# Attention in units of four key blocks, with paced row maxima, earlier output weights and operands loaded in place

## The chip, the cores and the metric

The program runs on one core of a Trainium2 chip (trn2). The metric is the device time of one execution in microseconds (us). A core has a matrix engine (TensorE, PE in the profile, with its weight loads as PEld), a vector engine (VectorE, DVE), a scalar engine (ScalarE, ACT) that also evaluates exp and tanh, a fourth engine (GpSimd, POOL) and a queue that issues the transfers between main memory and on-chip memory (SyncE, SP). Each engine takes its instructions in its program's order. Matmuls write to banks of PSUM; a "twin" is a pair of banks, one for each of the two heads that are worked together.

## The reference

One layer of a streaming encoder. After a modulated norm, one projection gives an S5 branch (a scan over the sequence and a gated linear unit, GLU) and an attention branch; both are gated, concatenated, and go through one output projection. The attention has 8 heads of 64, over a prompt of 2048 positions (causal) and over 64 new positions that see 512 cached ones.

```python
y_ssm = y_ssm * jax.nn.sigmoid(y_ssm @ w_glu.astype(f32) + b_glu.astype(f32))
y_ssm = (y_ssm * jax.nn.silu(z_s.astype(f32))).astype(x.dtype)
...
s = jnp.einsum('bqhd,bkhd->bhqk', q, k).astype(jnp.float32) * ATTN_SCALE
s = s + jnp.transpose(cum_q, (0, 2, 1))[:, :, :, None] - jnp.transpose(cum_k, (0, 2, 1))[:, :, None, :]
mask = pos_k[None, :] <= pos_q[:, None]
s = jnp.where(mask[None, None], s, -jnp.inf)
p = jax.nn.softmax(s, axis=-1)
return jnp.einsum('bhqk,bkhd->bqhd', p.astype(v.dtype), v)
```

## The kernel before

Four stages follow each other on PE: projections and scan (to 725 us), GLU (to 795), attention (to 1214), output product (to 1387). All matrix work is float32, made of products of a high and a low part.

**Attention** (class Attn) works on head pairs hp 0 to 3. Each has five query tiles: qt 0 to 3 of 512 prompt positions, and qt 4 for the new ones. `order` puts qt 4 first in each pair. A tile meets its key blocks of 128 keys; tile qt has 4·qt + 4 of them, and the last four (on the diagonal) are 512, 384, 256 and 128 queries wide. Each block passes through these steps, and the letters are used below:

- S, scores (`scores`): transposed scores (keys on partitions) in a twin, six matmuls in three pairs plus a pair (`sm`,`kb`) that adds the biases and subtracts the row maximum; ACT then writes exp into a block p (the `act` helper), and p is added to one of two running sums `acc` for the softmax's denominator, on DVE or POOL in turn (`i % 2`, recorded at L1489).
- V (`mix`): p times values into one PSUM bank, over all blocks of a tile. Two blocks (PVG = 2) make a unit; V of a unit is issued one unit later (`pend`).
- M, maxima (`maxima`): an upper bound of the next tiles' row maxima needs a coarse product q·k of 128 queries and up to 512 keys per twin, and DVE adds the biases `cb` and reduces (`pb`, `pm`, L1411; two per M). `run` issues one M after each S, whatever its size, while any are queued; their results go through a transpose (`identr`, `mq`) into `sm`.
- T (`turn`): PE transposes a loaded tile of k or q; ACT copies the high part, DVE subtracts for the low part (`ks`, `qs`, L1375).
- SUM (`sums`): the running sum's total over keys, its reciprocal, z (gate times result) and the store to `ma_d`.

PE's order is that of the code: the class Chain adds a dependency from each PE instruction to the one before. The other engines' order is set by a scheduler. PSUM holds three twins for S and M, one bank for V and one for T and SUM (`Banks`).

**GLU** (`Glu.mm`): 16 steps of 24 matmuls each. After ACT's tanh, two operations on DVE (L1663, L1664) form the product of the tanh, y and the gate. Two M and one T per step are put between (MXU = 2).

**Output** (class Out): `weights` is a generator that loads the 16 blocks of the output weights through a ring of three buffers `ost` (L1749), casts the high part on ACT (`ohb`, L319) and subtracts the low part on POOL (`olb`, L205). `run` of Attn advances it by two steps per unit, from the point at which no loads, transposes or maxima are left. Out.run then computes eight pairs of chunks with seven products each; `load`, `differ` and `split` bring, combine and split the operands of pair p; SP fetches stored weights (`t3`, `t4`) and residual rows x between them.

## Time and profile before

| | |
|---|---|
| median of 3 runs | 1392.0 us (1387.33 to 1394.06) |
| profiled execution, its own time | 1393.23 us |
| its span in the profile | 1391.4 us, 1.83 us outside |
| PE busy | 1312.5 us (94%) |
| DVE busy | 968.5 us (70%) |
| ACT busy | 652.0 us (47%) |
| POOL busy | 520.5 us (37%) |
| mean granted PE clock | 0.981 of full speed |

A busy time is the union of an engine's instructions; matmuls overlap in their pipeline, so the duration of one group of matmuls is longer than its distance to the next group's start. What a group costs on PE is therefore read from the starts of consecutive rows. In 795 to 1214.3, PE counts as busy for 400.77 of 419.30 us; a wait between two matmuls that is shorter than the pipeline's fill does not show as idle time.

### The profile page before, as it was taken

Reading aid. Unit: us, or ns where it says so; the run is one execution under the profiler, and the core shown is the slowest. Engines: PE = TensorE matmul, PEld = TensorE weight load, DVE = VectorE, ACT = ScalarE, POOL = GpSimd, SP = SyncE. Lnnn points to the kernel's source line nnn. Section 1 sums busy time; section 2 is a strip of 40 time slices with the busy share of each in tenths; the row PEclk is TensorE's granted clock in tenths of the full one; section 3 lists DMA queues with packets and bytes.
Section 4 is the critical chain, followed back from the end, with each engine's and each line's share of the span. In section 5 each row is a group of like instructions: output and inputs, shape, how many; then the busy total and the mean of one; then the engine's idle time right before and its main releaser. Section 6 shows DMA issues by size and latency. Waiting matters only on the chain.

```text
span 1391.4 us, 25886 instructions
## 1 busy us (share of the span) xinstructions
PE 1312.5 (94%) x9164; PEld 1031.9 (74%) x9164; DVE 968.5 (70%) x2404; ACT 652.0 (47%) x1710; POOL 520.5 (37%) x502
## 2 busy tenths in 40 slices
PE   5888999999999899999999899999999989898998
PEld 2886999998889899998879755555555554387887
DVE  3635896977877679864218877786787885446775
ACT  3645356567453576573315335445445445522211
POOL 1100254556534354452004113423423426743453
PEclk9899999999999999999999889999999999999999
DMA  9885333543546836446249624134121133495552
GB/s 342 318 309 124 100 86 94 154 123 107 163 133 217 282 110 180 145 141 196 84 138 291 202 73 121 32 91 125 43 70 48 40 65 79 146 330 169 182 164 78
DMA packets 249476, 204.92 MB, mean 147 GB/s; under 512 B 91296, under 2 KB 217340, under 8 KB 248322
## 3 DMA queue, kind: packets, MB, share of 16 engines
q1 hardware_dynamic: 249346, 203.27, 47.6%
q8 instruction: 72, 1.18, 0.4%
q14 instruction: 58, 0.48, 0.1%
HBM read 137.68 MB, written 65.53 MB: 146 GB/s over the span
## 4 chain that ended last, share of the span: by engine, by line
PE 63%; DVE 11%; DMA 6%; POOL 4%; issue 4%; ACT 3%; SPq 1%; DVEq 0%; ACTq 0%; POOLq 0%
PE low L154 25%; PE twin L154 13%; PE bank L154 12%; PE last L154 7%; PE glu L154 3%; DVE pb L1411 2%; PE bank L157 2%; DMA wst<-in_w_in_dram 1%; POOL qss L329 1%; POOL olb L205 1%; DMA lt<-t 1%; DVE acc L1489 1%; ACT p L354 1%; DVE ev L650 1%; DVE wlo L323 1%
## 5 line engine op out<-in xcount | busy, mean ns | idle before, releaser
L154 PE MATMUL low<-whi,h 128*128 128x256 f32 (+1 forms) x1584 | 296.3, 285 | 6.5 <-DVE th L609 3.5
L154 PE MATMUL low<-h,whi 128*128 128x256 f32 (+2 forms) x1152 | 277.6, 332 | 0.4 <-DVE h L323 0.3
L154 PEld LDWEIGHTS low<-whi,h 128*128 128x128 f32 x1584 | 247.9, 189 | 10.0 <-DVE th L609 3.7
L1411 DVE CUSTOM_DVE_ANT_0 pb<-twin,cb 128x512 bf16<-128x512 f32 (+3 forms) x328 | 199.9, 609 | 58.9 <-PE twin L154 49.1
L154 PE MATMUL low<-wlo,h 128*128 128x256 f32 (+1 forms) x816 | 229.1, 283 | 5.9 <-DVE wlo L323 5.9
L154 PEld LDWEIGHTS low<-h,whi 128*128 128x128 f32 x1152 | 195.5, 192 | 21.4 <-issue 2.8
L354 ACT ACTIVATE p<-twin 128x1024 f32<-128x1024 f32 (+3 forms) x180 | 149.7, 839 | 119.4 <-PE twin L154 107.2
L154 PE MATMUL low<-h,wlo 128*128 128x256 f32 (+2 forms) x576 | 188.2, 327 | 1.2 <-DVE wlo L323 1.2
L154 PEld LDWEIGHTS low<-wlo,h 128*128 128x128 f32 x816 | 154.3, 189 | 8.2 <-DVE wlo L323 7.7
L154 PE MATMUL bank<-p,vt 128*64 128x512 f32 (+3 forms) x704 | 142.5, 527 | 0.0
L154 PE MATMUL twin<-qs,ks 64*128 64x512 f32 (+3 forms) x1056 | 134.1, 359 | 0.0
L154 PEld LDWEIGHTS low<-h,wlo 128*128 128x128 f32 x576 | 110.3, 192 | 10.9 <-DVE wlo L323 2.6
L323 DVE TENSOR_TENSOR wlo<-wst,whi 128x512 fp32r<-128x512 f32 (+1 forms) x96 | 71.6, 752 | 59.9 <-ACT whi L319 59.7
L1489 DVE TENSOR_TENSOR acc<-acc,p 128x1024 f32<-128x1024 f32 (+4 forms) x88 | 90.2, 1025 | 30.5 <-ACT p L354 28.1
L329 POOL TENSOR_TENSOR qss<-qss,mhalf 128x4 f32<-128x4 f32 (+1 forms) x68 | 79.9, 1176 | 84.1 <-DVE qss L328 76.0
L154 PEld LDWEIGHTS twin<-qs,ks 64*128 64x128 f32 x1056 | 95.2, 191 | 11.0
L154 PE MATMUL twin<-sm,kb 64*128 64x512 f32 (+3 forms) x360 | 78.0, 428 | 21.2 <-DVE pm L1411 14.4
L319 ACT CAST whi<-wst 128x512 fp32r<-128x512 f32 (+1 forms) x96 | 58.7, 619 | 73.2 <-PE low L154 37.5
L154 PEld LDWEIGHTS bank<-p,vt 128*64 128x64 f32 x704 | 45.2, 140 | 63.8 <-issue 56.1
L205 POOL TENSOR_TENSOR x<-x,ot 128x512 f32<-128x512 f32 (+1 forms) x34 | 52.8, 1556 | 84.4 <-DVE ot L1816 79.7
L154 PEld LDWEIGHTS twin<-sm,kb 64*128 64x128 f32 x360 | 34.5, 187 | 61.8 <-DVE pm L1411 32.8
L646 ACT ACTIVATE hsq<-ev 128x64 bf16<-128x64 f32 (+1 forms) x272 | 69.7, 256 | 8.2
(437 smaller groups left out, 2634.2 us busy)
## 6 DMA issues: line engine op xcount, KB each, us to landing
wst<-in_w_in_dram SPq DMA_DIRECT2D x48, 512.0 KB
x<-in_x_prompt_dram SPq DMA_DIRECT2D x32, 512.0 KB
h<-h SPq DMA_DIRECT2D x16, 1024.0 KB
wada<-in_w_ada_dram SPq DMA_DIRECT2D x12, 1024.0 KB
cb<-cb_d SPq DMA_DIRECT2D x20, 512.0 KB
out_dram<-ev SPq DMA_DIRECT2D x64, 128.0 KB
out_dram<-x SPq DMA_DIRECT2D x32, 256.0 KB
z_d<-th SPq DMA_DIRECT2D x24, 256.0 KB
```

The source lines that it names most:

```text
L154: return self.keep(self.pe.matmul(*a, **kw))
L157: return self.keep(self.pe.transpose(*a, **kw))
L205: PL.tensor_tensor(out, x, y, op=op)
L319: i = S.copy(hi, x)
L323: V.tensor_tensor(lo, x, hi, op=ALU.subtract)
L329: PL.tensor_tensor(out, out, bc(mhalf[:out.shape[0]], list(out.shape)), op=ALU.pow)
L354: i = S.activation(out, x, func, **kw)
L646: S.activation(sq[:r], tv[:, h], AF.Square, accum_out=ss[:r, h:h + 1])
L650: V.tensor_tensor(tv, tv, e.bc(ss[:r].unsqueeze(2), [r, 4, HD]), op=ALU.mult)
L1411: V.tensor_tensor_reduce(b[:, :n], ps[:, h, :n], cb[:, h, :n], 1.0, NEG, ALU.add, ALU.max, accum_out=self.pm[:, t, h, pi:pi + 1])
L1489: (PL if j else V).tensor_tensor(y[:rows, :, c0:nq], x[:rows, :, c0:nq], p[:rows, :, :n], op=ALU.add)
```

## The change

Four parts, with the new names that matter.

**Units of four blocks.** PVG is 4, and V follows in the same unit, directly behind the unit's scores, with the blocks of the unit in order. The ring of p grows from 6 to 8 buffers, that of z from 2 to 3. The decode tile (qt 4) is no longer a row of units of its own: `decoded` makes its scores of four cached blocks in one twin with one exp, and it is joined to another unit (behind qt 1 for the first pair; with the last unit of the pair before for the others).

**Paced maxima.** `pace` issues an M only while DVE's estimated lag is below LAG or tiles need it: one at the head of a unit (none in the first unit), one in its middle, two behind its last scores. `biases` loads `cb` for each group of M (44 loads instead of 20, four buffers). Two transposes may share a twin (`turns`). The adds of a unit are issued behind its scores, three of eight on DVE and five on POOL (before, in turn), and smaller blocks may go to POOL too. DVE's order in attention is now pinned to the code's, by the same Chain class (so all its lines read L156).

**GLU.** The two DVE operations become two ACT operations, one POOL product (`pmul`) and one DVE product per step.

**Output weights and operands.** The weights start once nothing is left to load or transpose, though maxima may still be queued, with three steps per unit (four when no maxima are left), a ring of four, and the low part on DVE when no maxima are left. Operands of the first pairs are loaded in place, four `ot` instead of two; `load(2)` is issued before the residual's and `t4` fetches; decode's operands are split earlier.

```diff
-PVG = 2
+PVG = 4
 MXU = 2
+LAG = 4.6
...
-    def matmul(self, *a, **kw):
-        return self.keep(self.pe.matmul(*a, **kw))
-
-    def transpose(self, *a, **kw):
-        return self.keep(self.pe.transpose(*a, **kw))
+    def __getattr__(self, name):
+        f = getattr(self.pe, name)
+        return lambda *a, **kw: self.keep(f(*a, **kw))
...
+    V, PE = Chain(tc, nc.vector, nosync), Chain(tc, nc.tensor, nosync)
...
+            self.order += [(hp, qt) for qt in ((4, 0, 1, 2, 3) if hp else (0, 1, 4, 2, 3))]
...
+    def turns(self, two, apart):
+
+        n = self.due()
+        if n < 2 and not apart or not two:
+            return self.turn()
+        ps = self.twin()
+        self.evicts += [self.turned(False, ps[:, h]) for h in range(min(n, 2))]
...
+            if not self.can("cw" if new else "cb", 1):
+                return
+            w = DEC if new else 4 * P
+            t0 = 20 if new else 16 if kind == "c" else 4 * kind
+            cb = self.bias_at[j] = self.claim([P, 2, w], "cw" if new else "cb", j, F32)
+            e.nc.sync.dma_start(cb, e.cb_d[2 * hp:2 * hp + 2, t0 * P:t0 * P + w].partition_broadcast(P))
...
+    def pace(self, most=1):
+
+
+        for i in range(most):
+            if self.need <= 0 and self.lag >= LAG:
+                return i
+            n = self.maxima()
+            if not n:
+                return i
+            self.need -= 1
+            self.lag += 2 * n / 960 + 0.25 - n / 2400
+        return most
...
+        self.adds.append((tile, tile.n - 1, p, rows, c0, n))
+        return self.values[tile.hp, kd], t, rows, c0, n, p
+
+    def add(self, tile, i, p, rows, c0, n):
+
+        V, PL = self.e.V, self.e.PL
+        acc, nq = tile.acc, tile.nq
         whole = not c0 and rows == P
         late = tile.end and i >= tile.nb - 6
-        j = i % 2 if whole and not late else 0
+        j = int(i % 8 not in (0, 2, 5)) if not late and (whole or (acc[1] is not None and not tile.given[1])) else 0
+        if not j:
+            self.busy += 2 * n / 960 + 0.1
...
+            self.step()
+            self.busy = 0.0
+            self.need = 0
...
+                n = self.left(units[k][-1][0])
+                if n > 0:
+                    self.need = -(-n // max(1, k - at - 1))
+                    break
+            groups = []
+            if at:
+                self.pace()
...
+                for j, (kd, t) in enumerate(blocks):
+                    groups[-1].append(self.scores(tiles[i], kd, t))
+                    if j == 1 or j == 2 and self.need > 2:
+                        self.pace()
+            n = self.pace(2)
+            self.turns(n < 2 or len(unit) > 1, len(unit) > 1)
+            self.evict()
+            for x in self.adds:
+                self.add(*x)
+            self.adds = []
+            self.lag = max(0.0, self.lag + self.busy - 0.4 - sum(8.2 * x[4] for g in groups for x in g) / 2400)
+            for (i, blocks, first, last), group in reversed(list(zip(unit, groups))):
+                self.mix(tiles[i], group, first, last)
+            if len(unit) > 1:
+                self.end(tiles[unit[1][0]])
+                self.sums(tiles[unit[1][0]])
+            if len(unit) == 1:
+                if done:
+                    self.sums(done.pop(0))
...
+            if not (self.todo or self.loaded):
+                self.give(out)
+                for _ in range(4 if self.job == len(self.jobs) else 3):
                     next(weights, None)
...
-        e.V.scalar_tensor_tensor(x, x, 1.0, self.y[b], op0=ALU.add, op1=ALU.mult)
-        e.V.scalar_tensor_tensor(x, x, 0.25, self.z[b], op0=ALU.mult, op1=ALU.mult)
+            e.act(x[:, c], x[:, c], AF.Identity, scale=0.25, bias=e.quarter)
+        e.pmul(x, x, self.y[b])
+        e.V.tensor_tensor(x, x, self.z[b], op=ALU.mult)
...
-        yield from wait(5)
-        mem.ring("ost", 2048, 3)
+        yield from wait(6)
+        mem.ring("ost", 2048, 4)
...
+            e.split(st, h, l, el=e.V if self.idle() else None, keep=True)
...
-        for i in range(2):
-            m = self.a[0, "a%d2" % (i + 1)] = self.temp().rearrange("p (k c) -> p k c", k=4)
-            e.nc.sync.dma_start(m, e.ma_d[:, 0, P * i:P * i + P].rearrange("(k p) c -> p k c", p=P))
-        self.load(1, 1)
+        for t in range(2):
+            for i in range(2):
+                m = self.a[t, "a%d2" % (i + 1)] = self.temp().rearrange("p (k c) -> p k c", k=4)
+                e.nc.sync.dma_start(m, e.ma_d[:, t, P * i:P * i + P].rearrange("(k p) c -> p k c", p=P))
         for _ in weights:
             pass
+        self.load(2)
...
+        self.plain(0, 1, 1)
         self.differ(1, 2)
         self.differ(1, 4)
-        self.split(1, "a11", "s2")
-        self.plain(0, 1, 1)
         self.plain(0, 0, 1)
-        self.split(1, "s1", "a12")
+        self.split(1, "a12", "a11")
         self.plain(1, 1, 1)
-        self.split(1, "s3", "a22")
-        self.load(2)
+        self.split(1, "a22", "s2")
         self.plain(1, 0, 1)
+        self.split(1, "s1", "s3")
```

**How the order moves.** PE in the middle of attention, before: M and S alternate (sm, qs and ks stand for the operands of S and M: a twin from `ks`,`qs` is an M, one from `sm` and `qs` an S), and two blocks of V follow.

```order
L154 MATMUL twin_8163<-sm_4_8184,kb_0_7729 128x512 x2
L154 MATMUL twin_8163<-qs_8_8634,ks_4_8336 128x512 x2
L154 MATMUL twin_8163<-qs_8_8634,ks_5_8337 128x512 x2
L154 MATMUL twin_8163<-qs_9_8635,ks_4_8336 128x512 x2
L154 MATMUL twin_8167<-ks_12_8949,qs_4_8376 128x512 x2
L154 MATMUL bank_81<-p_3_9072,vt_2_9172 64x512 x2
L154 MATMUL bank_81<-p_4_9099,vt_2_9172 64x512 x2
L157 MATMUL bank_77<-ident_0_82,kn_1_8194 128x128 x4
L154 MATMUL twin_9004<-sm_4_8184,kb_0_7729 128x512 x2
```

The same place after: the two M at the end of a unit, a transpose, four blocks of V, a SUM, then the M of the next unit's head and its first S.

```order
L156 MATMUL twin_9081<-ks_8_8598,qs_4_8434 128x512 x2
L156 MATMUL twin_8181<-ks_8_8598,qs_4_8434 128x512 x2
L156 MATMUL bank_77<-ident_0_82,kn_0_8206 128x128
L156 MATMUL bank_81<-p_7_9238,vt_5_9972 64x512 x2
L156 MATMUL bank_81<-p_0_9098,vt_5_9972 64x512 x2
L156 MATMUL bank_81<-p_1_9112,vt_5_9972 64x512 x2
L156 MATMUL bank_81<-p_2_9134,vt_5_9972 64x512 x2
L156 MATMUL bank_77<-acc_3_9505,ones_0_91 64x512 x2
L156 MATMUL twin_8185<-ks_8_8598,qs_4_8434 128x512 x2
L156 MATMUL twin_9081<-sm_1_8196,kb_0_7731 128x512 x2
L156 MATMUL twin_9081<-qs_2_8220,ks_6_8437 128x512 x2
```

V stands in groups of four blocks where it stood in groups of two, and the M stand at the unit's two ends; over attention, the program has 40 groups of V where it had 91, 144 M where it had 150, and 108 transposes of k and q where it had 114 (six M and six transposes more are now issued in the GLU stage). DVE at such a place, before: the reductions of M (an ISA row each, and its accumulator row behind it) with single adds between.

```order
L1411 ISA pb_0_8412,pm_1_8546<-twin_9004,cb_2_8334 128x384
L1411 ISA pm_1_8546 128x1
L1489 TENSOR_TENSOR acc_2_9162<-acc_2_9162,p_2_9052 128x1024
L1411 ISA pb_0_8412,pm_1_8546<-twin_9004,cb_2_8334 128x384
L1411 ISA pm_1_8546 128x1
L1411 ISA pb_0_8412,pm_1_8546<-twin_9004,cb_2_8334 128x512
L1411 ISA pm_1_8546 128x1
```

After: M's reductions, then the low part of a transpose, two adds in a row, and the reductions of the next M.

```order
L156 ISA pb_0_8407,pm_0_8400<-twin_8181,cb_3_8228 128x512
L156 ISA pm_0_8400 128x1
L156 TENSOR_TENSOR ks_5_8320<-bank_77,ks_4_8319 128x512
L156 TENSOR_TENSOR acc_1_9248<-acc_1_9248,p_1_9112 128x1024
L156 TENSOR_TENSOR acc_1_9248<-acc_1_9248,p_3_9148 128x1024
L156 ISA pb_0_8407,pm_0_8400<-twin_8185,cb_3_8228 128x512
L156 ISA pm_0_8400 128x1
L156 ISA pb_0_8407,pm_0_8400<-twin_8185,cb_3_8228 128x512
```

The adds stand behind the unit's M and in front of the next, in a pinned order. SP in the output stage, before: the operands of pair 2 (`m`, from `ms_d` and `ma_d`) stand behind the `t4` fetches, x and three stores.

```order
L1807 DMA x_0_12890<-in_x_prompt_dram 128x1024
L1821 DMA out_dram<-x_1_12902 128x512 x2
L1821 DMA out_dram<-x_2_12904 128x512
L1827 DMA m_26112_0_12859<-ms_d 128x4x256
L1827 DMA m_30208_0_12942<-ma_d 128x4x256
L1821 DMA out_dram<-x_2_12904 128x512
```

After: they stand directly behind the `t3` fetches and in front of x, the stores and `late`.

```order
L1904 DMA ht_188672_0_13050<-t_68 128x512
L1904 DMA lt_190720_0_13051<-t_68 128x512
L2012 DMA m_68352_0_12952<-ms_d 128x4x256
L2012 DMA m_97024_0_13055<-ma_d 128x4x256
L1992 DMA x_3_13057<-in_x_prompt_dram 128x1024
L2006 DMA out_dram<-x_0_12967 8x8x512 x2
```

Between the two, the operands' loads pass 17 transfers of SP's queue.

## Rows read from the trace of the kernel before

**Rows 1.** Busy time by stretch: stretch and its length, then busy us (and instructions) of PE, PEld, DVE, ACT, POOL, then granted PE clock, DMA share and GB/s; the first row is the GLU stage, the last sums nine stretches from 795 to 1214.3.

```profile
720.00:795.00 75.00, 68.39 (x555) 61.81 (x554) 57.42 (x134) 32.02 (x63) 20.83 (x17) 0.98 0.79 242
...
795.00:822.00 27.00, 24.32 (x192) 15.52 (x189) 18.41 (x56) 9.06 (x17) 1.79 (x3) 0.74 0.44 118
822.00:904.00 82.00, 81.91 (x643) 44.04 (x639) 65.08 (x175) 40.46 (x52) 32.66 (x15) 1.00 0.26 74
904.00:924.00 20.00, 18.20 (x187) 11.53 (x187) 18.58 (x54) 9.16 (x16) 4.10 (x5) 1.00 0.30 72
...
1003.00:1024.00 21.00, 17.83 (x189) 10.77 (x187) 19.53 (x56) 7.68 (x17) 5.71 (x5) 1.00 0.31 83
...
1181.00:1214.30 33.30, 26.89 (x168) 12.62 (x164) 12.96 (x8) 19.60 (x29) 26.31 (x14) 0.90 0.46 140
sum 419.30, PE 400.77 PEld 221.28 DVE 311.17 ACT 204.66 POOL 163.93; mean PE 44.53 PEld 24.59 DVE 34.57 ACT 22.74 POOL 18.21
```

**Rows 2.** PE's timeline in the second head pair: start us, duration us, engine, line, operation, out<-in, shapes, count.

```profile
878.44 0.65 PE L157 MATMUL bank<-ident,kn 128*128 128x128 f32 x4
879.03 0.50 PE L154 MATMUL twin<-sm,kb 64*128 64x512 f32 x2
...
888.81 0.48 PE L157 MATMUL bank<-identr,mq 128*73 128x128 f32 x4
889.22 0.50 PE L154 MATMUL twin<-sm,kb 64*128 64x512 f32 x2
889.56 0.86 PE L154 MATMUL twin<-qs,ks 64*128 64x512 f32 x6
890.26 0.39 PE L154 MATMUL twin<-ks,qs 64*128 64x512 f32 x2
890.49 0.39 PE L154 MATMUL twin<-sm,kb 64*128 64x512 f32 x2
...
891.60 0.50 PE L154 MATMUL twin<-ks,qs 64*128 64x512 f32 x2
892.03 1.94 PE L154 MATMUL bank<-p,vt 128*64 128x512 f32 x8
893.90 0.49 PE L154 MATMUL twin<-sm,kb 64*128 64x512 f32 x2
894.24 0.85 PE L154 MATMUL twin<-qs,ks 64*128 64x512 f32 x6
```

**Rows 3.** PE's timeline in the last tiles of the third head pair, with the narrower blocks.

```profile
1169.92 0.51 PE L154 MATMUL twin<-qs,ks 64*128 64x256 f32 x6
1170.27 0.23 PE L154 MATMUL twin<-m_kq,identb 64*128 64x128 bf16 x2
...
1170.37 0.30 PE L154 MATMUL twin<-sm,kb 64*128 64x128 f32 x2
1170.51 0.50 PE L154 MATMUL twin<-qs,ks 64*128 64x128 f32 x6
1170.85 0.23 PE L154 MATMUL twin<-m_kq,identb 64*128 64x128 bf16 x2
```

**Rows 4.** Groups of instructions by form, 795 to 1215: line, engine, operation, names and shapes, count | busy us, mean ns | idle before and its releasers.

```profile
L1411 DVE CUSTOM_DVE_ANT_0 pb<-twin,cb 128x512 bf16<-128x512 f32 x209 | 143.6, 687 | 29.8 <-PE twin L154 23.8 <-DVE pm L1411 0.5 <-PE bank L154 0.3
L354 ACT ACTIVATE p<-twin 128x1024 f32<-128x1024 f32 x112 | 113.8, 1025 | 67.4 <-PE twin L154 64.2
...
L1489 POOL TENSOR_TENSOR acc<-acc,p 128x1024 f32<-128x1024 f32 x22 | 52.3, 2378 | 44.1 <-ACT p L354 44.1
L1489 DVE TENSOR_TENSOR acc<-acc,p 128x1024 f32<-128x1024 f32 x38 | 50.4, 1327 | 25.5 <-ACT p L354 23.7
...
L319 ACT CAST ohb<-ost 128x512 fp32r<-128x512 f32 x16 | 9.7, 617 | 18.7 <-DMA ost<-in_w_out_dram 18.7
```

**Rows 5.** Timeline of DVE: one add to a running sum.

```profile
950.73 1.23 DVE L1489 TENSOR_TENSOR acc<-acc,p 128x1024 f32<-128x1024 f32 x1
```

**Rows 6.** Timeline of POOL: the add that comes next.

```profile
952.00 2.37 POOL L1489 TENSOR_TENSOR acc<-acc,p 128x1024 f32<-128x1024 f32 x1 [1.42 <-ACT p L354]
```

**Rows 7.** What PE waited for: us in total, times, longest. The first row is of the GLU stage (720 to 795), the next two of attention (795 to 1214.3), the last of 1215 to 1290.

```profile
PE twin L154 <- DVE pm L1411: 4.3, 3, 3.2
...
PE twin L154 <- DVE pm L1411: 11.2, 14, 1.4
PE twin L154 <- ACT p L354: 6.4, 3, 2.6
...
PE last L154 <- DVE ot L1882: 3.7, 1, 3.7
```

**Rows 8.** Groups of instructions by form in the GLU stage, columns as in rows 4.

```profile
L205 POOL TENSOR_TENSOR yl<-yt,yh 128x528 fp32r<-128x528 f32 x12 | 18.4, 1557 | 28.1 <-PE glu L154 28.1
...
L1664 DVE SCALAR_TENSOR_TENSOR gx<-gx,gz 128x528 f32<-128x528 f32 x16 | 16.1, 1009 | 0.7 <-DMA gz<-z_d 0.6
...
L1663 DVE SCALAR_TENSOR_TENSOR gx<-gx,yt 128x528 f32<-128x528 f32 x16 | 14.2, 886 | 7.7 <-ACT gx L354 7.6
```

**Rows 9.** The chain of waits at the start of the output product: start us, us, what.

```profile
1250.22 7.14 DMA m<-ma_d
...
1263.80 5.49 PE last L154 x12
1269.29 2.98 PE bank L154 x12
```

337 lines of the change are left out of this document (215 added, 122 removed).

## The prediction

> **What bounds the kernel now.** I read the busy time by stretch first. In attention (795 to 1214.3) PE counts as busy for 400.77 of 419.30 us, and DVE for 311.17 [rows 1], so PE sets the pace. The stretches differ. From 822 to 904 PE is busy for 81.91 of 82.00 us and DVE for 65.08. Where one head pair gives way to the next, DVE is nearly full: 18.58 of 20 and 19.53 of 21 us in two such stretches, and PE falls to 18.20 and 17.83 [rows 1]. There the blocks are narrow, and an M comes with each S whatever its width, so DVE's reductions set the time. At the end (1181 to 1214.3) PE is busy for 26.89 of 33.30 us at a granted clock of 0.90, and at the start (795 to 822) the clock is 0.74 [rows 1].
>
> A busy time hides short waits, so I worked out what PE needs from the starts of consecutive rows. Six score matmuls take .70 us (889.56 to 890.26), a pair of M or of the bias .23 (890.26 to 890.49) [rows 2], so a full block of S takes .93. V of two full blocks takes 1.87 (892.03 to 893.90), four pairs of .467 [rows 2]. S of 256 and 128 queries takes .35 and .34 plus a pair of a third of that, so .47 and .45, and the masks take .10 (1170.27 to 1170.37) [rows 3]; S of 384 I put at three quarters of a full one, .70, and narrower V in proportion to their columns. Four transposes take .59 (878.44 to 879.03) and four of the maxima .41 (888.81 to 889.22) [rows 2]. V has a price of its own: the pair before it takes .43 (891.60 to 892.03) where the same pair takes .23, and the pair behind it .34 (893.90 to 894.24) [rows 2]. Entering and leaving V costs .20 and .11, together .31 us.
>
> The program has 112 full blocks of S (the rows hold their 112 exp [rows 4]), 16 of each of the three narrower widths, and 20 of decode, which are 128 wide. S: 112 × .93 + 16 × (.70 + .47) + 36 × .45 = 139. V: 112 × 1.87 / 2 = 105, and 27 for the narrower: 132. M: 150, of which 106 full at .23, with the narrower ones and their masks 36. Transposes of k and q: 114 × .15 = 17; of the maxima: 6; 20 SUM at .9 (a V pair with its turns): 18; masks of S: 6; entering and leaving V: 91 × .31 = 28. The sum is 382 us, and 419.3 are taken. So 37 us of the attention are waits of PE or a lower clock. The largest named ones are 11.2 us for DVE's `pm` and 6.4 for ACT's exp in three waits [rows 7].
>
> **The change part by part.**
>
> *Units of four.* 91 groups of V become 40, so 51 × .31 = 15.8 us of PE go. Six M at about .2 and six transposes at .15 move into the GLU stage: 2.2 us less here. Together 18. V now follows in its own unit. The last block's exp takes 1.03 us, and two M, a transpose and V of three earlier blocks (2.8 us) lie between on PE: I cost that at nothing; uncovered, it would be at most one exp (1.03) per unit, 41 in all. The decode tile joins another unit: its scores are unchanged, its four exps become one. 24 more loads of `cb` (512 KB each, 12.6 MB) add 33 GB/s to the 72 to 140 of these stretches, where the GLU stage moves 242 [rows 1]: nothing; if one is late, or values behind the decode tile's store in SP's queue, the M or V behind it wait, and less of the 37 us goes.
>
> *The waits.* The pacing removes the excess of DVE work in narrow units, and the low weights' casts leave the end. In a full unit PE needs 8 × .93 for S and V, .93 for four M, .31, and .6 for a transpose: 9.3 us. DVE needs four M of two reductions at .687 [rows 4] with their accumulator reads, 5.7; a low part, as wide as a reduction, .69; 1.25 adds at 1.23 [rows 5] (24 full ones and 26 narrower over 40 units), 1.5; some .3 else: 8.2 us. So a unit leaves DVE about 1.1 us, and the question is what comes late within it. DVE's order is now pinned, and behind its adds stand the reductions of the next unit's M, for whose twin PE waits two blocks of S later. Let w be the wait per unit over 40 units. The upper bound for one exposed add is a whole POOL add, 2.38 us [rows 4]; the lower is 0. DVE and POOL never work on two adds at once: DVE's at 950.73 lasts 1.23, and POOL's starts at 952.00, .04 us after its end [rows 5, 6]. A DVE add lasts 1.33 in the mean against 1.23 there [rows 4, 5], so today it waits little. POOL will hold more: 14 more adds at 2.38 and 20 narrower (3, 7 and 10 of the three widths, about 20 us), so 164 [rows 1] + 53 = 217 of some 386 us, .56 of the time. An add meets a running one with that chance and waits half of it, 1.19: .67 each, .83 per unit. The 1.1 us to spare hide part of it. I take .55, nearer to the 0 of today's rows than to 2.38; 40 × .55 = 22 stands in place of 37.
>
> The Trainium skill ("SBUF — State Buffer", section "Who interferes with whom") says that a DVE instruction with two SBUF inputs contends with a GpSimd instruction that reads SBUF, that the one which comes second blocks fully, and that issue order decides which. The trace agrees where DVE came first [rows 5, 6]; that DVE waits a whole POOL add no row here shows. By that rule at its worst, w = 2.38 and the sum is that of the third rival below.
>
> *Weights.* The casts `ohb` wait 18.7 us for their loads [rows 4] in ACT's order, where exp stands behind them; that gives the 6.4 us. Three steps per unit from an earlier point and a ring of four spread them. This is counted within the 37; if it fails, 6 come back.
>
> *GLU.* Two DVE operations of 886 and 1009 ns in the mean [rows 8] become one of about .69. DVE is freed of some 19 us over 16 steps, and pays 6 more M. PE waits 4.3 us for `pm` [rows 7]; that goes, and 2.2 of M and transposes come: 2 gained. The product on POOL is priced by `yl`, of the same shape, at 1557 ns [rows 8]; nothing on PE waits for it, since its result goes to a store. If the later `yl` of the next tile stood behind it, one such operation could be exposed at each of eight tiles: 12 us lost, the other end of that term.
>
> *Output.* SP issues the operands of pair 2 at 1250.22, the transfer takes 7.14, and PE waits 3.7 us for DVE's `ot`, which stands behind their `differ` in DVE's order; the 12 matmuls at 1263.80 then take 5.49 us where the next 12 take 2.98, at a lowered clock [rows 7, 9]. That is 6 us. In the new order 17 transfers are no longer ahead, and the wait is gone. If not, 0 is gained.
>
> The profiled execution took 1393.2 us, 1.2 above the median of the three runs; the sum is made against it. 1393.2 − 18 − 37 − 2 − 6 = 1330 with no wait left, so 1330 + 40 w. With w = .55 it is **1352**.
>
> **The rivals.**
>
> *No wait at all.* The 1.1 us to spare hide every port wait: 1330. For it: 822 to 904, where PE is full [rows 1]. Against it: the start at a lower clock (0.74) and the boundaries, whose M must be done on time.
>
> *The waits only move.* The units with the decode tile and narrow blocks are as full on DVE as before (18.58 of 20, 19.53 of 21), since every M must still be done before its tile; all 37 us stay: 1367, and with the weights' or GLU's term lost as well 1373 to 1384. For it: DVE's total falls little, 50 of its adds remain. Against it: M come at an even number per unit, not one per narrow block.
>
> *DVE waits for POOL in a pinned order: slower.* Place: the adds behind each unit's M, in front of the next M. Price: w up to 2.38. Decisive point: 1330 + 40 w = 1393 at w = 1.58. With a whole POOL add in each unit it is 1425. For it: POOL gets five of eight adds, two adds follow each other on DVE, and a scheduler can no longer move a reduction ahead of a waiting add. Against it: the first add waits at most what is left of a running one, and DVE has 1.1 us to spare.
>
> *The change gives no new cover for ACT.* The exp of the last block is exposed in each unit: 41 us, so 1371 without and 1393 with the other waits. Three V groups lie between, so I give this little.
>
> **How the numbers follow.** A difference of .5%, 7 us, is about what a measurement of this kernel can tell from none. The forecast (w from .2 to .92, 1338 to 1367) has .58; no wait .12; waits that move, with or without a lost term, up to 1384, .16; a result within 1385 to 1399 (w about 1.4 to 1.7, or the exposed exp) .05; slower by the port .09. Faster by over .5%: .58 + .12 + .16 = .86; within: .05; slower: .09. The range of 8 in 10 goes from 1330 to 1384: all of the forecast, half of the no-wait case and the moved waits.
>
> **What would show it.** V in groups of 16 matmuls in PE's timeline with .31 us about each; attention from 793 to about 1179; DVE's adds in it at more than 1.33 in the mean if the port bites, and then idle PE behind `pm`; no PE wait for exp near its end; DVE at about 43 us instead of 57.42 in the GLU stage [rows 1]; no wait of 3.7 at the output product's start. The prediction is wrong if PE waits more than .92 us per unit, or if the GLU stage becomes longer.

## The result, and the profile after

The change makes the kernel faster by about 1%: 1377.58 us in the median of six runs (1373.48 to 1380.54) against 1392.57 for the kernel before in the same comparison, a ratio of 0.9891 (95% interval 0.9864 to 0.9917). The time lies in the predicted range, by its number in the case "the waits only move"; 15 us were gained where 41 were forecast. The profiled execution took 1377.64 us with a span of 1375.6, 15.8 shorter than before, so the two traces can be laid side by side. One execution of a later kernel (`ends`), 4323.18 us where its other three took 1364.99 to 1370.18, is left out of that kernel's ratio.

First, when each stage starts on PE, by three marks: GLU's matmuls, attention's first score (a twin from `sm`,`kb`), and the output products with `mha` (in both kernels 32 other matmuls of the output stand ahead of them). In a row of a group, the start of its last matmul stands after "to". The kernel before:

```profile
L154 PE MATMUL glu<-yh,wgh x128: 280/284/393, 725.0 to 787.3; 128*128 128x264 f32 x128
...
792.30 0.48 PE L154 MATMUL twin<-sm,kb 64*128 64x128 f32 x2 [3.22 <-DVE pm L1411]
...
L154 PE MATMUL last<-ohb,mha x112: 389/389/794, 1224.5 to 1386.1; 128*128 128x512 f32 x112
```

The kernel after:

```profile
L156 PE MATMUL glu<-yh,wgh x128: 280/284/388, 726.5 to 790.9; 128*128 128x264 f32 x128
...
791.98 0.50 PE L156 MATMUL twin<-sm,kb 64*128 64x512 f32 x2
...
L156 PE MATMUL last<-ohb,mha x112: 388/389/395, 1214.8 to 1370.2; 128*128 128x512 f32 x112
```

The first GLU matmul starts 1.5 us later. From there to the first score GLU lasts 65.5 us instead of 67.3 (its matmuls alone span 2.1 us more, with six M and six transposes more between them); attention lasts 422.8 (792.0 to 1214.8) instead of 432.2 (792.3 to 1224.5), the output product 155.4 instead of 161.6. That is +1.5 −1.8 −9.4 −6.2 = −15.9, the whole difference. Of the forecast terms GLU's and the output's came as foreseen, and attention gave 9 instead of 33.

Next, busy time by stretch after, with the columns of [rows 1]: GLU, attention, and its first two head pairs; then the same of the kernel before.

```profile
722.00:793.00 71.00, 68.52 (x555) 61.02 (x553) 45.04 (x132) 45.07 (x94) 36.86 (x29) 1.00 0.83 254
...
791.20:1210.30 419.10, 392.72 (x3250) 227.88 (x3249) 299.75 (x737) 198.93 (x275) 209.98 (x112) 0.98 0.40 111
...
791.20:900.00 108.80, 103.63 (x885) 61.56 (x883) 75.41 (x197) 50.77 (x68) 49.43 (x27) 0.97 0.37 105
900.00:1001.60 101.60, 98.52 (x837) 57.66 (x837) 73.38 (x198) 49.60 (x68) 52.39 (x27) 1.00 0.41 113
```

```profile
787.70:1217.20 429.50, 406.68 (x3227) 225.50 (x3227) 318.90 (x803) 207.64 (x291) 163.93 (x87) 0.97 0.31 83
...
787.70:906.70 119.00, 112.44 (x884) 64.08 (x883) 90.89 (x250) 53.23 (x74) 35.18 (x18) 0.93 0.33 93
906.70:1009.50 102.80, 100.70 (x825) 56.94 (x825) 79.33 (x210) 51.29 (x71) 36.70 (x19) 1.00 0.32 87
```

In attention PE's busy time fell by 14.0 us (406.68 to 392.72), while its idle time rose from 22.8 to 26.4. Only the first head pair became shorter by much (119.0 to 108.8): 8.8 of the 14.0 us are in it (112.44 to 103.63), and there the granted clock rose from 0.93 to 0.97. The second gained 1.2, and its idle time grew from 2.1 to 3.1. DVE's 57.42 in GLU [rows 1] are 45.04 in a stretch 4 us shorter, so DVE was freed there as forecast, and PE's wait of 3.22 us ahead of the first score is gone.

What PE waited for in attention after, to hold against [rows 7]:

```profile
PE twin L156 <- DVE pm L156: 12.2, 22, 3.1
PE twin L156 <- ACT p L356: 5.7, 9, 1.3
PE bank L156 <- DVE z L156: 3.8, 4, 1.4
PE bank L156 <- DMA vt<-out_dram: 3.0, 3, 1.9
```

The wait for `pm` was 11.2 us in 14 cases and is 12.2 in 22. New are the waits of the bank for DVE's `z` and for values that arrive late (and .9 us for `sm`). Exp costs 5.7 instead of 6.4, but at other places: before, three waits in the last 33 us of attention; now nine, none of them there. The first of the three, and the last of the nine:

```profile
1184.54 0.79 PE L154 MATMUL twin<-sm,kb 64*128 64x512 f32 x2 [2.65 <-ACT p L354]
...
1157.13 0.50 PE L156 MATMUL twin<-sm,kb 64*128 64x512 f32 x2 [1.27 <-ACT p L356]
```

Groups by form in attention after, to hold against [rows 4]:

```profile
L1582 POOL TENSOR_TENSOR acc<-acc,p 128x1024 f32<-128x1024 f32 x36 | 90.7, 2519 | 20.6 <-ACT p L356 19.2
...
L156 DVE TENSOR_TENSOR acc<-acc,p 128x1024 f32<-128x1024 f32 x24 | 42.3, 1762 | 1.4 <-ACT p L356 0.8
...
L321 ACT CAST ohb<-ost 128x512 fp32r<-128x512 f32 x16 | 8.9, 614 | 0.0
```

DVE has 24 full adds instead of 38, but one lasts 1762 ns where it lasted 1327; POOL's has grown from 2378 to 2519. The casts `ohb` no longer wait for their loads (0.0 against 18.7).

Two places of the timeline after: a unit of the second head pair on PE, with DVE's eight reductions beside it; then a place in the last head pair where DVE adds while POOL subtracts, and PE waits.

```profile
932.83 0.44 PE L156 MATMUL twin<-ks,qs 64*128 64x512 f32 x2
933.47 0.50 PE L156 MATMUL twin<-sm,kb 64*128 64x512 f32 x2 [0.20 <-DVE pm L156]
...
934.50 0.40 PE L156 MATMUL twin<-ks,qs 64*128 64x512 f32 x2
935.07 0.51 PE L156 MATMUL twin<-ks,qs 64*128 64x512 f32 x2 [0.17 <-DVE pm L156]
935.51 0.66 PE L156 MATMUL bank<-ident,kn 128*128 128x128 f32 x4
936.10 3.65 PE L156 MATMUL bank<-p,vt 128*64 128x512 f32 x16
939.58 1.03 PE L156 MATMUL bank<-acc,ones 128*64 128x512 f32 x4
...
931.98 0.69 DVE L156 CUSTOM_DVE_ANT_0 pb<-twin,cb 128x512 bf16<-128x512 f32 x1
...
937.50 0.69 DVE L156 CUSTOM_DVE_ANT_0 pb<-twin,cb 128x512 bf16<-128x512 f32 x1
938.12 0.08 DVE L156 DVE_READ_ACCUMULATOR2_ANT pm<- 128x1 f32 x1
...
1162.29 5.94 DVE L156 TENSOR_TENSOR acc<-acc,p 128x1024 f32<-128x1024 f32 x3
1168.15 0.68 DVE L156 CUSTOM_DVE_ANT_0 pb<-twin,cb 128x512 bf16<-128x512 f32 x1
...
1162.32 3.50 POOL L205 TENSOR_TENSOR olb<-ost,ohb 128x512 fp32r<-128x512 f32 x2
...
1169.63 0.39 PE L156 MATMUL twin<-sm,kb 64*128 64x256 f32 x2 [3.12 <-DVE pm L156]
```

PE waits for DVE ahead of the score at 933.47 (.20) and of the second M at the unit's end (.17): the two M start .57 apart, at 934.50 and 935.07, where a pair takes .23 [rows 2]. DVE meanwhile runs reductions almost without a gap from 931.98 to 938.12: four M in 6.1 us, about 1.5 each, where PE needs .93 + .23 = 1.16 for a score and an M. V itself became cheaper, 16 matmuls in 3.48 us (936.10 to 939.58) where two groups of eight took 1.87 each [rows 2]. In the second place three adds last 5.94 us, nearly 2 each, while POOL holds two `olb`; the reductions stand behind them, and PE idles 3.12 us.

The chain of work early in the output stage, to hold against [rows 9]:

```profile
1251.03 2.72 PE last L156 x12
1253.75 2.72 PE bank L156 x12
```

These are the same two groups of twelve matmuls as in [rows 9]: no wait stands ahead of them now, and the first takes 2.72 us instead of 5.49.

### The profile page after: what moved, and what is told of

Same layout as the page of the kernel before. It is cut to its first block, busy times and chain, and to the rows that moved or that the text cites. A ratio compares the mean times of both kernels' runs of the same rounds, so it can differ in the third digit from the quotient of the medians.

```text
span 1375.6 us, 25961 instructions
## 1 busy us (share of the span) xinstructions
PE 1297.6 (94%) x9196; PEld 1034.1 (75%) x9196; DVE 948.8 (69%) x2361; ACT 658.9 (48%) x1730; POOL 585.2 (43%) x546
## 5 line engine op out<-in xcount | busy, mean ns | idle before, releaser
L156 PE MATMUL low<-whi,h 128*128 128x256 f32 (+1 forms) x1584 | 297.1, 286 | 5.6 <-DVE th L156 3.5
L156 PE MATMUL low<-h,whi 128*128 128x256 f32 (+2 forms) x1152 | 278.7, 333 | 0.4 <-DVE h L156 0.3
L156 DVE CUSTOM_DVE_ANT_0 pb<-twin,cb 128x512 bf16<-128x512 f32 (+3 forms) x328 | 200.6, 612 | 82.2 <-PE twin L156 66.4
L156 PEld LDWEIGHTS low<-whi,h 128*128 128x128 f32 x1584 | 248.8, 190 | 9.1 <-DVE th L156 3.9
L156 PE MATMUL low<-wlo,h 128*128 128x256 f32 (+1 forms) x816 | 229.5, 284 | 5.1 <-DVE wlo L156 5.1
L156 PEld LDWEIGHTS low<-h,whi 128*128 128x128 f32 x1152 | 196.5, 193 | 21.4 <-issue 2.8
L156 PE MATMUL low<-h,wlo 128*128 128x256 f32 (+2 forms) x576 | 188.7, 328 | 2.0 <-DVE wlo L156 2.0
L356 ACT ACTIVATE p<-twin 128x1024 f32<-128x1024 f32 (+3 forms) x164 | 142.1, 899 | 69.8 <-PE twin L156 68.4
L156 PEld LDWEIGHTS low<-wlo,h 128*128 128x128 f32 x816 | 154.9, 190 | 7.0 <-DVE wlo L156 6.5
L156 PE MATMUL bank<-p,vt 128*64 128x512 f32 (+3 forms) x704 | 134.4, 524 | 3.0 <-DMA vt<-out_dram 3.0
L156 PE MATMUL twin<-qs,ks 64*128 64x512 f32 (+3 forms) x1056 | 132.1, 356 | 0.0
L1582 POOL TENSOR_TENSOR acc<-acc,p 128x1024 f32<-128x1024 f32 (+3 forms) x56 | 112.4, 2006 | 32.3 <-ACT p L356 29.6
L156 PEld LDWEIGHTS low<-h,wlo 128*128 128x128 f32 x576 | 111.0, 193 | 11.4 <-DVE wlo L156 3.0
L156 DVE TENSOR_TENSOR wlo<-wst,whi 128x512 fp32r<-128x512 f32 (+1 forms) x96 | 71.3, 749 | 60.6 <-ACT whi L321 57.4
L156 PEld LDWEIGHTS twin<-qs,ks 64*128 64x128 f32 x1056 | 93.4, 188 | 12.2
L156 PEld LDWEIGHTS bank<-p,vt 128*64 128x64 f32 x704 | 46.6, 140 | 72.3 <-issue 62.6
L156 PE MATMUL twin<-sm,kb 64*128 64x512 f32 (+3 forms) x360 | 72.5, 398 | 11.4 <-DVE pm L156 5.2
L156 PE MATMUL twin<-ks,qs 64*128 64x512 f32 (+3 forms) x328 | 70.5, 435 | 8.6 <-DVE pm L156 7.4
```

Source lines behind the costliest of these rows:

```text
L156: return lambda *a, **kw: self.keep(f(*a, **kw))
L356: i = S.activation(out, x, func, **kw)
L1582: (PL if j else V).tensor_tensor(y[:rows, :, c0:nq], x[:rows, :, c0:nq], p[:rows, :, :n], op=ALU.add)
```

## The experiments

Three theories stood at the start. The port (A in the expectations where they use letters): DVE's adds wait for POOL, and in the pinned order the reductions wait behind them. DVE's load and order (B): even at full speed the adds and the reductions, in the order and place that they have, empty the twins late. And a third (C), that a group of V has no price of its own, so that nothing was to be gained by larger groups. Each ratio below is to the kernel before in the same batch, with its 95% interval; the changed kernel has 0.9891 [0.9864, 0.9917]. A hundredth is 13.9 us. A difference of two such ratios is uncertain by some 4 to 7 us either way, and the differences in us below are to be read so.

**The port, and the adds as a whole.** Adds to the running sums are left out, first POOL's, then DVE's.

```diff
+            if not j or x is not y:          (no_pool_adds)
+            if j or x is not y or late:      (no_dve_adds)
                 (PL if j else V).tensor_tensor(y[:rows, :, c0:nq], x[:rows, :, c0:nq], p[:rows, :, :n], op=ALU.add)
```

> The changed kernel, but 56 adds to running sums that it puts on POOL are left out (the 12 first ones of a tile and the 10 joins of two sums stay), and .25 is added before the logarithm, so the softmax's denominators are incomplete; DVE's list is the same. Theory A (port): DVE's adds wait for POOL's in a pinned order, 24 full ones took 1762 ns in the mean where one takes 1230 alone; with POOL's adds gone they take 1.23 to 1.3 us, DVE's pm come earlier and the time falls by 8 to 17 us, to 1361 to 1370. Theory B (bursts): DVE is late because three M stand close together at a unit's ends whatever POOL does; the time stays within 4 us of 1377.6. Theory C (V's price was too high): also within 4 us.

> The changed kernel, but DVE's adds to running sums are left out, save the first of each tile and those of the last two tiles' ends (and .25 is added before the logarithm), so the denominators are incomplete; POOL's list is the same. A and B both free DVE of some 45 adds (about 60 us with their waits): A: like the run without POOL's adds or somewhat more, 1357 to 1368; B: DVE's slack per unit doubles to 2.4 us, 1362 to 1370; C: within 4 us of 1377.6, since PE's own price is what is left.

Without POOL's adds: 0.9841 [0.9806, 0.9876], 1370.55 us. By form, DVE's full adds then read

```profile
L156 DVE TENSOR_TENSOR acc<-acc,p 128x1024 f32<-128x1024 f32 x24 | 30.3, 1263 | 8.1 <-ACT p L356 7.5
```

so POOL's adds stretch one of DVE's from 1263 to 1762 ns; that is real, and all that they cost is about 7 us, .2 per unit. One meeting in the changed kernel, where an add of DVE starts while POOL has two adds in a row, and ends 1.1 us after the second:

```profile
1053.75 2.98 DVE L156 TENSOR_TENSOR acc<-acc,p 128x1024 f32<-128x1024 f32 x1
...
1050.84 4.80 POOL L1582 TENSOR_TENSOR acc<-acc,p 128x1024 f32<-128x1024 f32 x2
```

Without DVE's adds: 0.9756 [0.9725, 0.9786], 1358.48 us, 19 us below the changed kernel. Its `pm` wait falls to 6.4 us, its `z` wait to 1.1, and the wait for values is gone. Most of what DVE's adds cost is therefore their own time, not POOL's hold on the port.

**The order of DVE, and where the adds stand.** One kernel takes the pinned order away, two move the adds of a unit: between the two M at its end, or behind the M at the next unit's head.

```diff
-        e.V.strict = True
+        e.V.strict = False                   (dve_free)
...
-            n = self.pace(2)
+            n = self.pace(1)
+            for x in self.adds:
+                self.add(*x)
+            self.adds = []
+            n += self.pace(1)                (adds_early)
...
+            self.flush()                     (adds_late: behind the next unit's first pace)
```

> The changed kernel with DVE's order left to the scheduler, which puts adds between the reductions as before. If the pinned order itself (adds in a row in front of the next M) makes PE wait, the time falls by 5 to 12 us, to 1366 to 1372. If it is the port or the M's place on PE, it stays within 4 us of 1377.6, or is longer.

> The changed kernel, with a unit's adds put on DVE between the two M at its end, not behind both and the low part. If what hurts is that adds stand in front of the next unit's M: the next M comes up to 1.4 us earlier per unit, time 1366 to 1373. If it is that adds in a pinned order stand in front of any M at all: within 4 us of 1377.6 or up to 15 us longer, as the second M now waits for exp and POOL.

> The changed kernel, but a unit's adds stand behind the M at the next unit's head, in DVE's and POOL's order (three and five of eight as it is). Putting adds ahead of the unit's last M cost 24 us, so their place in front of M is what hurts: if the same holds for the next unit's first M, the time falls by 4 to 10 us, to 1368 to 1374. If the wait then only moves to the M in the unit's middle: within 4 us of 1377.6. If p's buffers come free too late for the next exps: longer, with waits of ACT.

All three are slower, than the changed kernel and than the kernel before: 1.0221 [1.0181, 1.0261] free, 1.0061 [1.0038, 1.0084] early, 1.0156 [1.0119, 1.0193] late. Wherever the adds leave the shadow of V (the stretch of DVE's time that V covers on PE), some result that PE needs at once stands behind them: PE waits for `pm` (42.1 us free, where the scheduler moves more than the adds, and 39.4 late), or for the low parts `ks` and `qs` (14.9 and 7.5 early). So the pinned order, which the third rival blamed, is what holds the loss down. A stretch of the late kernel shows why the loss is larger than the waits:

```profile
1000.00:1050.00 50.00, 41.52 (x367) 26.30 (x363) 34.75 (x79) 18.05 (x27) 18.43 (x11) 0.85 0.32 87
```

PE idles 8.5 of 50 us there, and its granted clock falls to 0.85, so that the matmuls between the waits are slower too.

**The place and number of the M.** M behind every score instead of two at the end; units of two blocks in the changed kernel.

```diff
-            if at:
-                self.pace()
...
-                    if j == 1 or j == 2 and self.need > 2:
+                    if j < 3:
                         self.pace()
-            n = self.pace(2)
+            n = self.pace()                  (spread)
...
-PVG = 4
+PVG = 2                                      (pvg2)
```

> The changed kernel, with the M spread: one behind each of a unit's four scores, none at its head and one, not two, at its end. Theory B (three M close together at a unit's turn make DVE late): PE's waits for pm fall from 12 us to 6 or less and the time by 5 to 10 us, to 1368 to 1373. If the place of the M is not the cause (DVE's adds are): within 4 us of 1377.6, or longer, since an M's twin is then asked for sooner after the last.

> The changed kernel with units of two blocks (81 groups of V instead of 42), all else as it is. By the prediction's price of .31 us per group: 39 x .31 = 12 us longer, 1389.7. Theory C, that most of this price returns at other changes of operands: 1378 to 1382. If units of four also bring the M's bursts (B), units of two space them out: 1374 to 1380.

Spread: 0.9952 [0.9936, 0.9968], about 9 us slower than the changed kernel, with 51 short waits for `pm` (21.4 us) instead of 22 (12.2). Even spacing over the scores does not shorten them. Not all of the loss is theirs, for one long wait is new, near the end of attention, for a tile's row maxima (`mq`) that come too late with fewer M per unit:

```profile
PE bank L156 <- DVE mq L156: 6.2, 1, 6.2
```

Units of two: 1.0315 [1.0283, 1.0347], 44 us slower than the kernel before, which has units of two as well. Its pacing, boundary and pinned adds don't suit short V: `pm` 32.3 us, `z` 9.7, values 7.0.

**DVE's share of the adds.** Two of eight instead of three, in the changed order and in the late one.

```diff
-        j = int(i % 8 not in (0, 2, 5)) if ...
+        j = int(i % 8 not in (0, 2)) if ...
```

> The changed kernel, with two of eight adds on DVE and six on POOL (three and five). Leaving out all of DVE's adds gave 19 us, leaving out POOL's 7. If DVE's load is what counts, a third fewer adds on DVE give 4 to 6 us: 1371 to 1374. If the port counts as much, since POOL is busier by some 30 us: within 3 us of 1377.6. If POOL's sums become late for the SUM: longer.

> As adds_late, with two of eight adds on DVE and six on POOL. If place and load add up (6 us by the share alone): 1362 to 1368. If both remove the same waits: 1367 to 1372.

Two of eight give 0.9841 [0.9815, 0.9867], 7 us less than the changed kernel; in the late order 1.0137 [1.0097, 1.0177], no different from late alone. The load counts, but the place counts more.

**Weights and GLU, one by one.** The weights wait until no maxima are left; GLU's two DVE operations return.

```diff
-            if not (self.todo or self.loaded):
+            if not (self.todo or self.loaded or self.smq) and self.job == len(self.jobs):   (weights_late)
...
-            e.act(x[:, c], x[:, c], AF.Identity, scale=0.25, bias=e.quarter)
-        e.pmul(x, x, self.y[b])
-        e.V.tensor_tensor(x, x, self.z[b], op=ALU.mult)
+        e.V.scalar_tensor_tensor(x, x, 1.0, self.y[b], op0=ALU.add, op1=ALU.mult)
+        e.V.scalar_tensor_tensor(x, x, 0.25, self.z[b], op0=ALU.mult, op1=ALU.mult)          (glu_old)
```

> The changed kernel, but the output weights start only when no maxima are left, as before (with the new ring and four steps per unit). If the earlier start costs by its casts on ACT and low parts on POOL, which meet DVE's adds in the last head pair (three adds took 5.94 us there): 3 to 8 us faster in the last head pair, minus what the casts then cost at its end, 1370 to 1377. If the earlier start gains what was forecast (the 6.4 us of waits for exp come back): 1381 to 1390.

> The changed kernel with the two DVE operations per step of the GLU stage as before, and their ACT and POOL replacements gone. The stage's DVE waits fell from 4.3 to .9 us in the changed kernel. If that is worth what was forecast, the time grows by 2 to 5 us, to 1380 to 1383; if the stage is bound by PE's own work in both, it stays within 2 us of 1377.6.

0.9877 [0.9844, 0.9909] and 0.9907 [0.9874, 0.994]: both intervals hold the changed kernel's ratio. Neither part is worth anything that the total times can tell; for the weights it stays open on which side of zero. For GLU the trace tells more. From the first GLU matmul to the first score, with the old operations and then in the changed kernel, and PE's wait with the old ones:

```profile
722.60:791.50 68.90, 65.00 (x535) 58.27 (x535) 59.04 (x147) 30.18 (x62) 18.43 (x12) 1.00 0.84 257
...
726.50:792.00 65.50, 64.42 (x535) 58.18 (x535) 44.35 (x131) 43.47 (x93) 35.87 (x27) 1.00 0.87 267
...
PE twin L156 <- DVE pm L156: 3.5, 5, 1.6
```

The same 535 matmuls take 68.9 us with the old operations and 65.5 with the new, where PE waits .9 us for `pm`. So freeing DVE is worth some 3 us in the stage, in one trace of each; the stretch ahead of GLU differs by more than that between the two traces (it ends at 722.6 and 726.5), and so hides it in the totals.

**The boundary between head pairs.** The two new waits have one place: decode's SUM is written into the bank of its V and waits for DVE's `z`, and the values of the next pair stand in SP's queue behind decode's store. This kernel puts that SUM in a twin and issues the values ahead; the next one adds two of eight.

```diff
-        pt = self.f.tile([P, 512], F32, tag="tr", name="sum") if tile.qt < 4 else e.psum[0][:, P:2 * P]
+        pt = self.f.tile([P, 512], F32, tag="tr", name="sum") if tile.qt < 4 else self.twin()[:, 0]
...
+            for x in units[at + 1] if at + 1 < len(units) else ():
+                self.vload(x[0])
             for (i, blocks, first, last), group in reversed(list(zip(unit, groups))):
```

> The changed kernel, with the SUM of the decode tile in a twin, not in the bank of its V, and the next tile's values issued on SP ahead of the decode tile's store. The trace of the changed kernel has 3.8 us of PE waiting for z (four times) and 3.0 for values (three times). If these are waits on the path: both gone, 1370 to 1373. If DVE is what ends last there anyway: within 3 us of 1377.6.

> The changed kernel with both repairs: the decode tile's SUM in a twin, values issued ahead of its store, and two of eight adds on DVE, six on POOL. The runs alone gave 8 and 6 us. If they remove different waits: 1363 to 1365. If both shorten what DVE's lateness costs: 1366 to 1369.

The first: 0.9831 [0.9786, 0.9877], 8 us less. PE's waits in it:

```profile
PE twin L156 <- DVE pm L156: 16.7, 24, 3.1
PE twin L156 <- ACT p L356: 4.2, 7, 1.3
PE twin L156 <- ACT sm L1396: 0.9, 2, 0.7
```

`z` and the values are gone (6.8 us in the changed kernel), while `pm` grew by 4.5; the gain of 8 us is uncertain by 7. Together with two of eight: 0.9819 [0.9788, 0.9851], 1367.32 us, the lowest ratio here of a kernel that leaves nothing out, though the intervals don't part it from either repair alone. The two gains of 8 and 7 give 10 together, so they seem to overlap; the intervals don't settle it.

> As ends62, with the M of a unit at its head, behind its second and third scores, and one at its end, so that no two M follow each other. If the second of two M in a row waits for its twin in each unit (.2 to .5 us over 40 units): 8 to 15 us faster than ends62, 1350 to 1357. If an M between scores only takes the twin that the next scores need, as in the run with spread M: 2 to 10 us slower than ends62.

> As ends62, with the output weights started only when no maxima are left. Alone it gave 3 us. With fewer adds on DVE the meeting of its adds with the low parts on POOL matters less: within 3 us of ends62. If POOL, now with six of eight adds, is late in the last head pair: 3 to 8 us faster than ends62.

On top of it, one M at the end of a unit and one more within (`n = self.pace()`, and an M behind the second and third score) gives 0.9908 [0.988, 0.9937], 12 us slower: no two M follow each other, yet `pm` costs 18.6 us instead of 14.3, and one wait for `mq`, as in the run with spread M, 7.2. The later weights give 0.9837 [0.9805, 0.9869], the same.

**The price of V alone, and who collects it.** Four kernels in a square, all made from the kernel before: V in groups of two or four (47 groups of V in place of 91; of the rest of the change only the eight buffers p and four steps of weights per unit; one spare buffer for `cb` instead of three), and DVE's reductions whole or over their last 128 columns.

```diff
-PVG = 2
+PVG = 4
...
+                self.turn()
+                self.step()                  (b_four: a transpose and a load ahead of V, SUM behind it)
...
-            V.tensor_tensor_reduce(b[:, :n], ps[:, h, :n], cb[:, h, :n], 1.0, NEG, ALU.add, ALU.max,
+            l = max(0, n - P)
+            V.tensor_tensor_reduce(b[:, l:n], ps[:, h, l:n], cb[:, h, l:n], 1.0, NEG, ALU.add, ALU.max,   (half)
```

> The kernel before with V in groups of four blocks and nothing else of the change: p has 8 buffers, cb one instead of three extra, an M still follows each S, POOL takes every other add, DVE's order is the scheduler's, the two transposes of a unit stand in front of and behind its V. PE goes over from S and M to V, SUM or transposes 49 times instead of 93. By the prediction's price of .31 us: 44 x .31 = 13.6 us faster than before, about 1378, as fast as the whole change. If the price is right but DVE's waits grow with the longer V as they did in the change: 1384 to 1392. If the price is not there: 1392.

> The kernel before, with each M's reductions reading only the last 128 columns (maxima incomplete; the exp gets a scale of .25 so that it stays finite): an M then costs DVE about .75 us where a full one costs 1.5. All matmuls, adds and loads stay. PE's waits for pm (14 us) mostly go, and with them some of the lowered clock: 1365 to 1382.

> The same cut of the reductions in b_four (V in groups of four in the old kernel, 66 us slower than it as it stands). If those 66 us are DVE, which no longer catches up in a V between two M and so empties the twins late: the wait for pm falls from 53 us to under 10, and this run is 8 to 14 us faster than b_half, 44 x .31 being the price of the changes that it spares. If four blocks in a row lose the time in another way (p's buffers, ACT's exps, cb): it stays over 20 us slower than b_half. If the price of .31 is not there: within 4 us of b_half.

| ratio to the kernel before | reductions whole | reductions cut |
|---|---|---|
| V in groups of two | 1 | 0.9856 [0.9831, 0.9882] |
| V in groups of four | 1.0472 [1.0442, 1.0502] | 0.9866 [0.9844, 0.9889] |

Groups of four cost 66 us with whole reductions and nothing that can be told with cut ones. With whole ones PE waits for `pm` like this between 793 and 1215, where the kernel before has 11.2 us in 14 waits [rows 7]:

```profile
PE twin L154 <- DVE pm L1411: 49.7, 55, 2.0
```

With cut ones, busy time over attention and in its middle, first in groups of two, then in groups of four; both first rows hold the same 3227 matmuls:

```profile
783.80:1193.20 409.40, 396.84 (x3227) 220.84 (x3225) 227.75 (x802) 207.43 (x290) 163.59 (x87) 0.99 0.33 87
...
820.00:1125.00 305.00, 304.68 (x2523) 171.35 (x2519) 174.90 (x677) 152.72 (x210) 110.39 (x58) 1.00 0.29 74
```

```profile
783.80:1192.40 408.60, 390.10 (x3227) 227.24 (x3225) 237.94 (x802) 205.41 (x291) 168.22 (x87) 0.98 0.32 85
...
820.00:1125.00 305.00, 296.68 (x2503) 172.12 (x2501) 179.06 (x661) 149.09 (x207) 114.71 (x58) 1.00 0.29 76
```

In groups of two PE is full in the middle (304.68 of 305 us), in groups of four it idles there for 8.3 us, and attention is shorter by only .8 us (409.40 to 408.60). PE's busy time for the same matmuls falls by 6.7 us, .15 for each of 44 groups; its clock was 0.98 against 0.99, so the price itself may be somewhat higher, and short waits count as busy, so some of it may be those. What PE saves it waits: its idle time grows from 12.6 to 18.5 us, 6.1 of it for `pm` (.9 in groups of two). So the third theory, that nothing is saved, falls, and larger groups still bring nothing where DVE fills the gap.

## Why the prediction was partly wrong

The time fell into the predicted range by luck: the case that has its number, "the waits only move", needs the weights' or GLU's term to be lost, and neither was; and it leaves attention the 18 us of V, where attention gave 9.

- **Units of four, 18 us of PE work: wrong as a gain, and open in size.** PE's busy time in attention fell by 14.0 us, or 17 without the 13 output matmuls (.23 each) that the later window holds and the earlier has one of. But 8.8 of the 14.0 us came in the first head pair, where the granted clock rose from 0.93 to 0.97, so a part of it is the clock. How much of that is the price of V's groups stays open between the .15 of the square and the .31 read from [rows 2]. The step was wrong in taking it as separable from the waits. V is also the time in which DVE empties the three twins: with V every two blocks, a group of V stands between the M; with V every four, scores and M follow each other at 1.16 us on PE while DVE needs 1.5 per M. The square shows it: the same regrouping costs 66 us with whole reductions and nothing with cut ones.
- **The waits, 37 gone and 22 in their place: the step that failed.** The 37 were the sum of work, 382, against the 419.30 us of a window that leaves out 10 us of attention (3.2 of them the wait ahead of the first score, which stands in GLU's term). And the sum was low: with DVE's reductions cut (an M then costs DVE about .75 us, less than the 1.16 of PE), the same matmuls keep PE busy for 396.84 us at a clock of 0.99. What cutting them gave was 18 us (attention of 432.2 against 414.1 by the marks above, in the kernel with cut reductions: 786.6 to 1200.7), and not 37. Of PE's idle time the change gave back nothing: it rose by 3.6 us in attention (22.8 to 26.4), and attention gave 9 us where 33 were forecast. By the prediction's own 1330 + 40 w, 1377.6 means w = 1.19 instead of .55, beyond the .92 that it named as its sign of being wrong. How the remainder of the old 47 us (429.5 less 382) divides between the lowered clock at the start and end [rows 1] and work summed too low, no run here separates.
- **DVE's spare 1.1 us per unit: the reason for that.** It was worked out as an average over a unit, 9.3 against 8.2, but the order within the unit decides. The 8.2 was low as well: four M took 6.1 us in the stretch above, not 5.7, and a full add 1.76, not 1.23. The scores before V and the M with them are DVE's busy part, and the adds belong behind the last M, in V's shadow; moved elsewhere, by hand or by the scheduler, they cost 24 to 46 us more. At the place they have, DVE's adds still cost 19.
- **The port: there, and smaller than priced.** .83 us per unit was put down for it, hidden in part; adds do last 1762 ns instead of the 1327 of [rows 4], and taking POOL's adds away gives 7 us, .2 per unit. The rows read for it ahead [rows 5, 6] didn't show it: POOL's row names exp as what it waited for, and that exp ran from 950.83 to 951.85. The third rival had the mechanism right (three adds in 5.94 us, PE idle for 3.12 behind them) and the size wrong, since few such meetings stand in front of a reduction that PE is about to need (the next longest wait for `pm` in attention is 1.6 us). The rule quoted in the prediction from the Trainium skill ("SBUF — State Buffer", "Who interferes with whom") agrees with the rows of the changed kernel, the add at 1053.75 above all, which takes 1.75 us more than one alone; the longest of the 24 takes 3.37. They do not show an add waiting a whole POOL add in each unit; the mean of 24 is .5 above the 1263 ns.
- **The SP queue and the decode tile, priced at nothing: wrong.** The prediction named the case, values behind the decode tile's store, and gave it no cost; it and SUM's wait for `z` are worth 8 us (1 to 16).
- **exp of the last block, at nothing: right.** V waits for late values alone, never for exp; the nine waits for exp (5.7 us) stand ahead of scores and M, for a twin. So the fourth rival did not come.
- **Weights: right in place, without a gain that shows.** The casts' 18.7 us of waiting are gone as forecast, and so are the three waits for exp near attention's end (6.4 us); in the kernel with later weights three stand there again (1.40, .67 and 1.90 us, from 1177.54 on). But its time is the same, and nine waits at other places, 5.7 us, came with the change.
- **GLU, 2 gained: right.** DVE was freed, the wait for `pm` fell from 4.3 us to .9, six M and six transposes came in, and the first score comes 65.5 us after the first GLU matmul instead of 67.3. The old operations in the new kernel bring the wait back (3.5) and make the stage 3.4 us longer.
- **Output, 6 gained: right.** 6.2; the wait of 3.7 us is gone, and the twelve matmuls behind it take 2.72 us instead of 5.49.

## What to carry to other kernels

A price read from a timeline can be right and still buy nothing: before spending it, ask what another engine does in the time that it removes, here DVE's emptying of the twins during V. To find whether a group's price or a second engine holds the time, shorten the second engine's work until it no longer holds the first, and try both groupings, as in the square above. Judge an in-order engine by what stands in front of each result that PE needs, not by its average slack, and take the window of a sum from the same first to last instruction as the work that is summed.

## What the runs showed of the hardware that was not expected

DVE and POOL slow each other both ways: DVE's full add goes from 1263 to 1762 ns when POOL adds too, and POOL's from 2387, in the kernel without most of DVE's adds, to 2519:

```profile
L1583 POOL TENSOR_TENSOR acc<-acc,p 128x1024 f32<-128x1024 f32 x36 | 85.9, 2387 | 23.8 <-ACT p L356 22.4
```

And long, frequent waits of PE went with a lower granted clock, so that they cost more than their length (the twelve matmuls of [rows 9], behind a wait of 3.7 us, took 5.49 us at a granted clock of 0.50; at 1.00 they take 2.72). Stretches of attention in the kernel with groups of four and whole reductions:

```profile
870.00:920.00 50.00, 43.65 (x306) 23.82 (x306) 33.62 (x84) 18.04 (x26) 16.82 (x8) 0.88 0.10 25
920.00:970.00 50.00, 42.95 (x330) 24.77 (x328) 33.40 (x91) 19.67 (x29) 10.36 (x7) 0.88 0.27 67
...
1020.00:1070.00 50.00, 41.98 (x336) 26.30 (x338) 33.66 (x96) 16.97 (x27) 10.48 (x7) 0.86 0.21 49
1070.00:1125.00 55.00, 48.41 (x391) 27.14 (x389) 37.59 (x100) 24.90 (x35) 17.51 (x9) 1.00 0.27 74
```

Where PE idled 6 to 8 of 50 us, the granted clock was 0.86 to 0.88, so it spent part of these stretches at the lower of its two levels (1.2 GHz of 2.4); in the last it idled 6.6 of 55 and kept 1.00, so the idle share alone does not tell when.
